# An encoder layer on one core: halved transposes and later squares at the output projection, one more FFN operand made there, and the FFN's first weights in other tiles

## The chip, the cores and the metric

The kernel runs on one core of one Trainium2 chip. The metric is the device time of one execution in microseconds (us). Engines are named as in the profile: PE is TensorE (PEld its weight loads), DVE is VectorE, ACT is ScalarE, POOL is GpSimd, SP is SyncE, which here only issues DMAs.

## The reference, cut to what matters

One layer is applied to a prompt of 2048 rows and to 8 x 16 sample rows (17 tiles of 128 rows; the samples are tile 16). After chunk-band attention and an mLSTM, their outputs are projected and added, and a gated FFN with a causal convolution of width 3 follows, all in float32:

```python
def layer(x, ...):
    h = rms_norm(x, norm_g[0])
    z = h @ w_in                                  # 1024 -> 3592
    ...                                           # att: band attention, mlstm_out: matrix memory
    mix = jnp.concatenate([att, mlstm_out], axis=-1) @ w_out          # 1024 -> 1024
    x = x + rms_norm(mix, norm_g[1])              # "x2" below
    ffn, new_buf = conv_ffn(rms_norm(x, norm_g[2]), conv_buf, w_up, w_conv, b_conv, w_down)
    return x + rms_norm(ffn, norm_g[3]), ...

def conv_ffn(h, buf, w_up, w_conv, b_conv, w_down):
    u = h @ w_up                                  # 1024 -> 5632
    ext = jnp.concatenate([buf, u], axis=1)
    y = b_conv
    for j in range(3):
        y = y + ext[:, j:j + S] * w_conv[j]
    gate, up = jnp.split(y, 2, axis=-1)
    return (gelu(gate) * up) @ w_down, ext[:, S:] # 2816 -> 1024
```

## The kernel before, in words

**Precision.** PE multiplies in fp32r, so every float32 operand is split into a high part (a cast on ACT) and a low part (the operand less its high part, on DVE), and every product is three matmuls: `mm3` issues high x high (L111), high x low (L112) and low x high (L113). A low part is thus wanted right after its high part.

**Stages.** First `w_in` with attention and mLSTM mixed in, then the output projection (`project`), then the FFN in three blocks of rows: block 0 is tiles 0 to 5, block 1 tiles 6 to 11, block 2 the rest. Each block has an up stage over 22 pairs of columns (order 0, 11, 1, 12, ...) and a down stage.

**Output projection.** `project` runs over tiles 0 to 7, 16, 8 to 15. For each it loads the row tile `mr`, normalises half of it, transposes it on PE in eight 128 x 128 pieces (`turn_rows`, which calls `rows_to_T`: PSUM tile `mT_pt`, high part by L218 on ACT and low part by L219 on DVE into `mt`), and multiplies `mt` by `w_out` in two column halves of 24 matmuls each (PSUM tiles `wo_0`, `wo_1`; group `wo`). The result goes through L1057 (DVE, times the norm's gains, into `mx`), L1059 (ACT, the squares), POOL (`rsqrt_mean`) and L1069 (DVE), and is stored as `x2d` (L1070). The code asks for the next tile's transposes after the first column half. `rows_to_T` takes four transposes to a PSUM tile of 512 columns, but all eight to one of 1024 columns if its bank is `ps_big`; tiles 0 to 7 use `ps_mm` (two buffers, which the `wo` sums use too), tiles 16 and 8 to 15 use `ps_big`. In the same time `folds` makes sums of `w_down` on DVE from pieces loaded and stored by POOL's DMAs (groups `fold`, `wtd`).

**FFN operands.** The up stage multiplies 2 x 2 blocks in seven products (P1, P6, P7, P5, then P2, P4, P3, in this order, as Strassen does), each by an operand `B` made of transposed normalised x2. While `project` works on its later tiles, the first block's operands are made by `h2_units(0)` in three units of two tiles: load x2 (`x2r`), squares (L1128, ACT), scale (L1132, DVE), four groups of four transposes (`h2T_pt`, PSUM `ps_sm`, two buffers), and pieces of 512 columns in the ring `quad` ("q", 11 buffers). `EARLY_B = 3`: P1, P6 and P7 are split into `B` at once; the raw pieces of P5, P2, P4 and P3 are stored to DRAM (`lated`) and, when the projection's weights give their space free, loaded again and split whole by `late_B` (L1198 on ACT, L1199 on DVE, 1536 columns each).

**FFN weights.** `load_up` loads the four blocks of `w_up` for a pair of columns; for block 0 it makes the sums s1 to s4 on DVE (L1371) and stores them (`wsd`) for the later blocks. Group n = 0 of a pair of columns has the weights of P1, P6, P7 and P5 (a11, s2, s3, s1), group n = 1 those of P2, P4 and P3 (a12, a22, s4). The split weights (L1353 on ACT, L1354 on DVE) go to `wuh`/`wul` in the pool tags "wh" and "wl" (two buffers each, which `project` uses for `mt` and `mx`) or to the tag "w3" (a set of four tiles in pool `p4`), in turns of three. `low[-1]` is the last low part issued.

**Order.** A list scheduler orders each engine's queue when the kernel is built; what is written earlier goes first where it is ready in the scheduler's own timing. Each engine, SP included, then runs its queue in order. DMAs marked `keep_in_program_order` are not moved. Pool `p4` and the tag "B" tiles in it lie where `w_out` stood (pool `phT`), `p3` lies where the attention's tiles stood (`p1`), and opens before tile 8.

Of the kernel before, what the change touches and what calls it, by code (L numbers as in the profile page):

```python
# [10 lines left out]
F32 = mybir.dt.float32  # L11
# [6 lines left out]
P = 128  # L18
# [3 lines left out]
DB = 8  # L22
# [6 lines left out]
NF = 22  # L29
# [21 lines left out]
def hymba_step(ctx: ExitStack, tc: tile.TileContext, I: dict, O: dict):  # L51
# [97 lines left out]

    gates = const.tile([P, 17, 8], F32, name="gates")  # L150

# [345 lines left out]
    def attention(pair, half):  # L497
        for kg in (2 * half, 2 * half + 1):
            for hh in range(2):
# [4 lines left out]

    tri = const.tile([P, P], F32, name="tri")
    nc.gpsimd.memset(tri, 1.0)
    nc.gpsimd.affine_select(out=tri, in_=tri, pattern=[[1, P]], compare_op=ALU.is_ge, fill=0.0, base=0,
                            channel_multiplier=-1)
    ind = const.tile([P, DB], F32, name="ind")
    nc.gpsimd.memset(ind, 1.0)  # L510
# [443 lines left out]
    wo = []  # L954
    g1 = []
    gatt = const.tile([P, 4], F32, name="gatt")

# [40 lines left out]
    def project(tiles):  # L998
# [27 lines left out]
        def turn_rows(s):  # L1026
            rows_to_T(s.m, s.mt, 0, f"mT{s.t}", ps_mm if s.t < 8 else ps_big)

# [48 lines left out]
    P1, P6, P7, P5, P2, P4, P3 = range(7)  # L1077
    EARLY_B = 3
    ffn = SimpleNamespace(B=[None] * 7, p4=None)

    def open_ffn():
# [10 lines left out]
    def quad(name):  # L1092
        return ffn.p3.tile([P, 512], F32, tag="q", name=name, bufs=11)

# [7 lines left out]
    def h2_units(b, between=(), lead=0):  # L1102
# [3 lines left out]
        def unit(halves, col, n, nm):  # L1106

            rows_ = {}
            for t, _ in halves:
                if t not in rows_:  # L1110
                    rows_[t] = row(f"x2r{t}") if late else rows_tile("xr", [P, D], f"x2r{t}")
                    fetch = nc.sync.dma_start(rows_[t], x2d[t])
                    if late:
                        tc.keep_in_program_order(fetch)
            yield 0.0, 0.0
            if not late:
                yield 0.0, 0.0
# [73 lines left out]

    def late_B():

        for i in (P5, P2, P4, P3):
            new_B(i, 0)
            hi, lo = ffn.B[i][:, 0], ffn.B[i][:, 1]
            nc.sync.dma_start(lo.bitcast(F32), lated[i - EARLY_B])
            nc.scalar.copy(hi, lo.bitcast(F32))  # L1198
            nc.vector.tensor_tensor(lo, lo.bitcast(F32), hi, op=ALU.subtract)  # L1199
# [186 lines left out]
    def load_up(b, i, g, quads=None):  # L1386
        f = ORDERS[b][i]
        n = 2 * i + g
        nm = f"{b}_{f}_{g}"
        if n % 3 < 2:  # L1390
            h = wpool.tile([P, 2112], F32R, tag="wh", name=f"wuh{nm}", bufs=2)
            l = wpool.tile([P, 2112], F32R, tag="wl", name=f"wul{nm}", bufs=2)
            at = [(h[:, i * 512:(i + 1) * 512], l[:, i * 512:(i + 1) * 512]) for i in range(4)]
        else:
            t = [p4.tile([P, 1056], F32R, tag="w3", name=f"wu3{nm}_{i}", bufs=4) for i in range(4)]
            at = [tuple(t[2 * x + i // 2][:, i % 2 * 512:i % 2 * 512 + 512] for x in range(2)) for i in range(4)]
# [95 lines left out]
    pend = [load_up(0, 0, 0)]  # L1492
    late_B()
    pend.append(load_up(0, 0, 1))
    g3 = norm_row(3)
    wcv = p4.tile([P, 44, 4], F32, tag="wcv", name="wcv")
# [13 lines left out]
    for b, tiles in enumerate(FBLOCKS):  # L1510
# [215 lines left out]
        if fast:  # L1726
# [3 lines left out]
            if last:  # L1730
                for i in range(2):
                    sets[i][1] = ps_sm(f"dns{b}_{i}")
                place = lambda pool, i: pool.tile([P, 3, D], F32, tag=f"B{i}", name=f"last{i}", bufs=1)
                fa, xa, fb, xb = place(p3, 0), place(p3, 1), place(p4, 3), place(p4, 4)
                F_ = [fa[:, 0], fa[:, 1], fb[:, 0], fb[:, 1], fa[:, 2]]
# [95 lines left out]
            for p, (_, _, set_, onto) in enumerate(SEQUENCE):  # L1831
                for c in range(3):
# [5 lines left out]
                    elif not last:  # L1838
                        quads = [load_quads(b + 1, 0, i) for i in range(2)]
                        pend = [load_up(b + 1, 0, 0, quads[0])]  # L1840
                    if last and c == 1 and p < 5:
# [37 lines left out]
            while ahead.step():  # L1879
                pass  # L1880
            pend.append(load_up(b + 1, 0, 1, quads[1]))
            continue
        for dh in range(2):
# [9 lines left out]
            for c in range(6):  # L1893
# [5 lines left out]
                elif not last:  # L1899
                    quads = [load_quads(b + 1, 0, i) for i in range(2)]  # L1900
                    pend = [load_up(b + 1, 0, 0, quads[0])]
                ks = list(range(4 * c, 4 * c + (4 if c < 5 else 2)))
# [52 lines left out]
        if not last:  # L1955
            while ahead.step():
                pass
            pend.append(load_up(b + 1, 0, 1, quads[1]))
    nc.sync.dma_start(O["conv_prompt"], halo)
# [94 lines left out]
```

## Time and profile before

| | |
|---|---|
| median of 3 runs (lowest to highest) | 2720.67 us (2716.08 to 2727.13) |
| the profiled execution: its time | 2719.23 us |
| its span, from first to last instruction | 2717.5 us |
| PE busy | 2647.4 us (97%), 16459 matmuls |
| DVE, ACT, POOL busy | 1863.2 (69%), 1422.9 (52%), 693.8 us (26%) |
| granted PE clock, mean | 0.994 |

A row of a view that groups instructions names line, engine, operation and the tiles (out<-in, buffer numbers left out), then the count, busy time and mean duration, and behind the last bar the idle time of the engine just before these instructions, and what ended it. In a timeline the bracket holds the same for one stretch. Matmuls are pipelined: a matmul of 512 columns shows 0.4 us, but the next one starts before it ends, so the spacing of starts is the better measure.

### The profile page before, as it was taken

The numbers are of one execution on the slowest core, as the hardware profiler recorded it, in microseconds if no ns is written. First come the engines' busy times: TensorE is split into PE (matmuls) and PEld (weight loads), VectorE is DVE, ScalarE is ACT, GpSimd is POOL, SyncE is SP. The second block draws the span as 40 slices with busy tenths as digits, with TensorE's granted clock in tenths as the row PEclk, the third lists the DMA queues.
The fourth block names the chain that finished last, engine by engine and source line by source line (L and its number), as shares of the span: only waits on it lengthen the run. The fifth ranks groups of instructions, "written<-read, shape, count | busy, mean of one in ns | idle before, by whom it ended". The sixth has DMA issues, their size and how long they took to land. (4 is left out here: it accounts for less than half of the span.)

```text
span 2717.5 us, 47627 instructions
## 1 busy us (share of the span) xinstructions
PE 2647.4 (97%) x16459; PEld 2475.1 (91%) x16459; DVE 1863.2 (69%) x3519; ACT 1422.9 (52%) x2904; POOL 693.8 (26%) x1325
## 2 busy tenths in 40 slices
PE   7999999999999999999999999999999999999998
PEld 7899989998999998777999997889999888999987
DVE  5444555433556666566899998758888775899866
ACT  4455554433556665333554556654554665555555
POOL 1000001201000001354454542013333212465501
PEclk9999999999999999999999999999999999999999
DMA  5545465458644555588777668767786777788695
GB/s 174 159 123 150 126 184 159 151 157 261 190 141 129 157 147 158 187 291 290 283 235 231 204 199 284 242 195 201 223 221 192 225 251 249 205 246 245 197 345 175
DMA packets 333855, 555.73 MB, mean 205 GB/s; under 512 B 61906, under 2 KB 169518, under 8 KB 333294
## 3 DMA queue, kind: packets, MB, share of 16 engines
q1 hardware_dynamic: 250942, 405.06, 48.0%
q0 software_dynamic: 44080, 113.81, 14.6%
q10 hardware_dynamic: 38592, 33.83, 3.7%
q8 instruction: 129, 2.11, 0.3%
q14 instruction: 112, 0.92, 0.1%
HBM read 390.03 MB, written 172.22 MB: 207 GB/s over the span
## 5 line engine op out<-in xcount | busy, mean ns | idle before, releaser
L111 PE MATMUL uec<-B,wuh 128*128 128x384 f32 (+1 forms) x720 | 235.9, 328 | 6.4 <-DVE ug L1527 4.7
L112 PE MATMUL uec<-B,wuh 128*128 128x384 f32 (+1 forms) x720 | 235.1, 327 | 0.0
L113 PE MATMUL uec<-B,wul 128*128 128x384 f32 (+1 forms) x720 | 234.4, 327 | 0.0
L1353 ACT CAST wuh<-wu 128x512 fp32r<-128x512 f32 x255 | 141.6, 618 | 114.7 <-PE uec L112 110.4
L1354 DVE TENSOR_TENSOR wul<-wu,wuh 128x512 fp32r<-128x512 f32 x255 | 164.3, 683 | 3.0 <-ACT wuh L1353 2.4
L111 PE MATMUL vo<-wi_h,hT 128*128 128x256 f32 x544 | 156.5, 288 | 1.6 <-ACT vo_st L244 1.6
L113 PE MATMUL dn<-wdh,al 128*128 128x512 f32 x385 | 154.5, 401 | 1.0 <-DVE al L1354 0.9
L113 PE MATMUL vo<-wi_h,hT 128*128 128x256 f32 x544 | 155.2, 285 | 0.0
L112 PE MATMUL vo<-wi_l,hT 128*128 128x256 f32 x544 | 155.0, 285 | 0.0
L111 PE MATMUL dn<-wdh,ah 128*128 128x512 f32 x385 | 152.8, 397 | 1.7 <-ACT wdh L1353 1.6
L1354 DVE TENSOR_TENSOR wdl<-wdr,wdh 128x512 fp32r<-128x512 f32 x231 | 145.6, 685 | 9.8 <-ACT wdh L1353 7.8
L112 PE MATMUL dn<-wdl,ah 128*128 128x512 f32 x385 | 151.6, 394 | 0.0
L111 PEld LDWEIGHTS uec<-B,wuh 128*128 128x128 f32 x720 | 135.1, 188 | 9.4 <-issue 4.4
L423 ACT ACTIVATE tmp<-tmp,mn 128x640 f32<-128x640 f32 (+4 forms) x128 | 97.6, 763 | 86.7 <-DVE mn L422 73.9
L422 DVE CUSTOM_DVE_ANT_0 tmp<-s,nb 128x640 f32<-128x640 f32 (+4 forms) x128 | 94.1, 737 | 65.7 <-PE s L412 65.3
L1353 ACT CAST wdh<-wdr 128x512 fp32r<-128x512 f32 x231 | 128.3, 620 | 17.2 <-PE uec L112 7.9
L112 PEld LDWEIGHTS uec<-B,wuh 128*128 128x128 f32 x720 | 135.2, 188 | 0.2
L113 PEld LDWEIGHTS uec<-B,wul 128*128 128x128 f32 x720 | 135.1, 188 | 0.0
L435 DVE TENSOR_TENSOR ptl<-pt,pth 128x640 fp32r<-128x640 f32 (+4 forms) x128 | 93.7, 738 | 58.4 <-ACT pth L434 57.7
L1354 DVE TENSOR_TENSOR al<-ar,ah 128x768 fp32r<-128x768 f32 (+1 forms) x104 | 80.5, 785 | 75.8 <-ACT ah L1353 75.5
L111 PE MATMUL qb<-hT,wi_h 128*128 128x384 f32 (+1 forms) x384 | 128.7, 335 | 0.0
L111 PE MATMUL qk<-hT,wi_h 128*128 128x384 f32 (+1 forms) x384 | 128.0, 333 | 0.6 <-ACT gates L293 0.5
(488 smaller groups left out, 9075.7 us busy)
## 6 DMA issues: line engine op xcount, KB each, us to landing
wu<-in_w_up SPq DMA_DIRECT2D x220, 256.0 KB, 4.8
wu<-wsd SPq DMA_DIRECT2D x176, 256.0 KB, 4.7
wdr<-wtd SPq DMA_DIRECT2D x132, 256.0 KB, 5.9
wi_raw<-in_w_in SPq DMA_DIRECT2D x52, 512.0 KB, 4.1
wdr<-in_w_down SPq DMA_DIRECT2D x99, 256.0 KB, 4.3
wsd<-ws POOLq DMA_DIRECT2D x88, 256.0 KB, 4.8
ar<-ad_S SPq DMA_DIRECT2D x40, 384.0 KB, 3.8
kraw<-kTd SPq DMA_DIRECT2D x112, 128.0 KB, 3.2
```

The source lines that it names most:

```text
L111: nc.tensor.matmul(out, ah, bh, start=start, stop=False, skip_group_check=onto)
L112: nc.tensor.matmul(out, ah, bl, start=False, stop=False, skip_group_check=onto)
L113: nc.tensor.matmul(out, al, bh, start=False, stop=stop, skip_group_check=onto)
L422: nc.vector.tensor_tensor_reduce(o_, s_, b_, 1.0, 3e38, ALU.add, ALU.min, accum_out=mn)
L423: nc.scalar.activation(tmp[:, :n], tmp[:, :n], AF.Exp, bias=mn, scale=-1.0, accum_out=rsum[:, i % 4, hh:hh + 1])
L435: nc.vector.tensor_tensor(s.ptl[:, sl, qc], ptv, s.pth[:, sl, qc], op=ALU.subtract)
L1353: nc.scalar.copy(h, r)
L1354: low.append(nc.vector.tensor_tensor(l, r, h, op=ALU.subtract))
```

## The change: what it does

It does these things:

1. `turn_rows` uses `ps_mm` for tiles 0 to 3 alone (`TURN_BIG = 4`). For the others each group of four transposes takes the first half of a `ps_big` buffer of its own, and L218 and L219 take 512 columns at a time.
2. In `h2_units(0)` the squares of a unit come four steps after the loads of its x2 rows, where it was one.
3. `EARLY_B = 4`: P5's operand is split during the projection too, and lies in `p3`. Three tensors `lated` are left.
4. To make room in `p3`, three of the eleven `quad` buffers lie in `p4` once that exists, and eight in `p3`; `gates`, `tri` and `ind` move from the pool `const` into `pm`, which closes before the FFN.
5. The handoff from the projection to the FFN is written in another order: weights n = 0, then P2's operand, then weights n = 1, then P4's and P3's operands behind the last of these weights. In block 0 the tag "w3" now takes the groups n % 3 == 1 (but the last), "wh"/"wl" the others; in the later blocks it is as before.

```diff
-    gates = const.tile([P, 17, 8], F32, name="gates")
+    gates = pm.tile([P, 17, 8], F32, tag="gates", name="gates", bufs=1)
...
+    TURN_BIG = 4
...
-            rows_to_T(s.m, s.mt, 0, f"mT{s.t}", ps_mm if s.t < 8 else ps_big)
+            rows_to_T(s.m, s.mt, 0, f"mT{s.t}", ps_mm if s.t < TURN_BIG else lambda name: ps_big(name)[:, 0:512])
...
-    EARLY_B = 3
+    EARLY_B = 4
...
     def quad(name):
-        return ffn.p3.tile([P, 512], F32, tag="q", name=name, bufs=11)
+        quads[0] += 1
+        if ffn.p4 is None or quads[0] % 11 < 8:
+            return ffn.p3.tile([P, 512], F32, tag="q", name=name, bufs=8)
+        return ffn.p4.tile([P, 512], F32, tag="q4", name=name, bufs=3)
...
-            yield 0.0, 0.0
-            if not late:
+            for _ in range(4 if late else 2):
                 yield 0.0, 0.0
...
-    def late_B():
-        for i in (P5, P2, P4, P3):
+    def late_B(*which):
+        for i in which:
...
-        if n % 3 < 2:
+        if n % 3 != (2 if b else 1) or n == 2 * NF - 1:
...
     pend = [load_up(0, 0, 0)]
-    late_B()
+    late_B(P2)
     pend.append(load_up(0, 0, 1))
+    with tc.issue_after(low[-1].ins):
+        late_B(P4, P3)
...
-                fa, xa, fb, xb = place(p3, 0), place(p3, 1), place(p4, 3), place(p4, 4)
+                fa, xa, fb, xb = place(p3, 0), place(p3, 1), place(p3, 3), place(p4, 4)
```

The same parts of `gates` hold for `tri` and `ind`; a local list `quads` of the down stages is renamed `raw_up`. In the changed kernel most lines behind `TURN_BIG` stand 1 to 6 lines lower (L1057 is L1058 there, L1353 is L1357).

**The order on the engines.** The rows are those of the built programs, as far as the text speaks of them. First PE where the first unit of `h2_units(0)` begins (`x2r` are its rows), before the change: each group of its transposes stands between matmuls of the projection.

```order
L113 MATMUL wo_1_14868<-wo_13521,mt_14684 128x512
L111 MATMUL wo_1_14868<-wo_13622,mt_14684 128x512
L1140 MATMUL h2T_pt_0_0_14859<-ident,x2r_14769 128x128 x4
L112 MATMUL wo_1_14868<-wo_13622,mt_14684 128x512
L113 MATMUL wo_1_14868<-wo_13622,mt_14684 128x512
```

With the change the unit begins a tile later; three of its four groups and the eight transposes of tile 10 (`mT_pt`) stand in a row between tile 9's last matmul and tile 10's first ones (`mt_14909`), and the two column halves of tile 10 take turns.

```order
L113 MATMUL wo_1_15006<-wo_13622,mt_14788 128x512
L1144 MATMUL h2T_pt_0_0_14933<-ident,x2r_14775 128x128 x4
L1144 MATMUL h2T_pt_1_0_14959<-ident,x2r_14777 128x128 x4
L1144 MATMUL h2T_pt_1_1_14990<-ident,x2r_14777 128x128 x4
L83 MATMUL mT_pt_14974<-ident,mr_14849 128x128 x4
L83 MATMUL mT_pt_14981<-ident,mr_14849 128x128 x4
L1144 MATMUL h2T_pt_0_1_15024<-ident,x2r_14775 128x128 x4
L111 MATMUL wo_0_15069<-wo_13346,mt_14909 128x512
L112 MATMUL wo_0_15069<-wo_13346,mt_14909 128x512
L111 MATMUL wo_1_15134<-wo_13346,mt_14909 128x512
L112 MATMUL wo_1_15134<-wo_13346,mt_14909 128x512
L113 MATMUL wo_0_15069<-wo_13346,mt_14909 128x512
```

The next place is DVE at the transposes of tile 16 (`mt_14574`). Before, its low part, in one instruction, stood behind three additions of `folds`:

```order
L1057 TENSOR_TENSOR mx_14582<-wo_1_14642,norm_row_13058 128x512
L1213 TENSOR_TENSOR fold_2_14395<-fold_0_14330,fold_2_14395 128x512
L733 TENSOR_TENSOR num_14_14159<-num_14_14159,ms_14_1_14186 128x129
L1213 TENSOR_TENSOR fold_3_14397<-fold_3_14397,fold_2_14395 128x512
L667 SCALAR_TENSOR_TENSOR ad_14_14231<-num_14_14159 128x2
L219 TENSOR_TENSOR mt_14574<-mT_pt_14615,mt_14574 128x1024
L668 TENSOR_TENSOR ad_14_14231<-ad_14_14231,colsp 128x2
```

With the change it is in two halves, the first behind one addition:

```order
L1217 TENSOR_TENSOR fold_3_13975<-fold_3_13975,fold_2_13973 128x512
L219 TENSOR_TENSOR mt_14574<-mT_pt_14615,mt_14574 128x512
L722 TENSOR_TENSOR w_14_0_14121<-ms_14_0_14118,w_14_0_14121 128x128
L219 TENSOR_TENSOR mt_14574<-mT_pt_14622,mt_14574 128x512
L1058 TENSOR_TENSOR mx_14582<-wo_1_14645,norm_row_13058 128x512
```

The last place is the handoff, first on DVE, from the last tile's second column half (`mx_15651` before, `mx_15682` now) on. `wul_0_0` are the low parts of weights n = 0, `B_0` the operands of `late_B`. Before:

```order
L1057 TENSOR_TENSOR mx_15651<-wo_1_15684,norm_row_13058 128x512
L1354 TENSOR_TENSOR wul_0_0_15730<-wu_0_15731,wuh_0_0_15729 128x512
L1354 TENSOR_TENSOR wul_0_0_15730<-ws_1_15740,wuh_0_0_15729 128x512
L1354 TENSOR_TENSOR wul_0_0_15730<-ws_2_15741,wuh_0_0_15729 128x512
L1354 TENSOR_TENSOR wul_0_0_15730<-ws_0_15739,wuh_0_0_15729 128x512
L1354 TENSOR_TENSOR wu_11_0_2_15792<-wu_0_15794,wu_11_0_0_15790 128x512
L1371 TENSOR_TENSOR ws_0_15802<-wu_3_15800,wu_2_15798 128x512
L1069 SCALAR_TENSOR_TENSOR mx_15651<-mx_15651,n_15_rs 128x1024
L1371 TENSOR_TENSOR ws_1_15803<-ws_0_15802,wu_0_15794 128x512
L1371 TENSOR_TENSOR ws_2_15804<-wu_0_15794,wu_3_15800 128x512
L1199 TENSOR_TENSOR B_0_15759<-B_0_15759 128x1536
L1679 TENSOR_TENSOR x_0_0_15826<-x_0_0_15825,ub_0_15823 128x384
```

Now three of the four low parts of n = 0 stand ahead of the last tile's instruction, the sums `ws_2` and `ws_3` (whose buffers lie in `p4`) behind it, and the first `B_0` and the last tile's L1070 come after the split of weights n = 1 (`wu_0_1`):

```order
L1358 TENSOR_TENSOR wul_0_0_15761<-wu_0_15762,wuh_0_0_15760 128x512
L1358 TENSOR_TENSOR wul_0_0_15761<-ws_1_15771,wuh_0_0_15760 128x512
L1358 TENSOR_TENSOR wul_0_0_15761<-ws_0_15770,wuh_0_0_15760 128x512
L1058 TENSOR_TENSOR mx_15682<-wo_1_15715,norm_row_13058 128x512
L1375 TENSOR_TENSOR ws_2_15772<-wu_0_15762,wu_3_15768 128x512
L1375 TENSOR_TENSOR ws_3_15773<-wu_1_15764,ws_1_15771 128x512
L1358 TENSOR_TENSOR wu_0_1_2_15796<-wu_1_15764,wu_0_1_0_15794 128x512
L1358 TENSOR_TENSOR wu_0_1_2_15796<-wu_2_15766,wu_0_1_0_15794 128x512
L1375 TENSOR_TENSOR ws_0_15829<-wu_3_15827,wu_2_15825 128x512
L1358 TENSOR_TENSOR wul_0_0_15761<-ws_2_15772,wuh_0_0_15760 128x512
L1358 TENSOR_TENSOR wu_0_1_3_15797<-ws_3_15773,wu_0_1_1_15795 128x512
L1685 TENSOR_TENSOR x_0_0_15853<-x_0_0_15852,ub_0_15850 128x384
```

And SP's queue at the handoff. Before, the four loads of `lated` stood behind tile 14's store of x2:

```order
L1043 DMA mx_15651<-in_x_prompt 128x1024
L1366 DMA wu_2_15798<-in_w_up 128x512
L1366 DMA wu_3_15800<-in_w_up 128x512
L1070 DMA x2d_279<-mx_15550 128x1024
L1197 DMA B_0_15759<-lated_261 128x1536
L1197 DMA B_0_15763<-lated_262 128x1536
L1197 DMA B_0_15767<-lated_263 128x1536
L1197 DMA B_0_15771<-lated_264 128x1536
L105 DMA norm_row_15783<-in_norm_g 128x1024
L1497 DMA wcv<-in_w_conv 128x176
L1499 DMA sext<-in_cache_conv 128x704
L1070 DMA x2d_280<-mx_15651 128x1024
```

Now a load of the second pair's weights, `wu_3_15827`, stands ahead of them. Its buffer is that of a sum of weights n = 0, so it waits for the third `wul_0_0` row of DVE's list above and for POOL's store of that sum:

```order
L1044 DMA mx_15682<-in_x_prompt 128x1024
L1071 DMA x2d_279<-mx_15578 128x1024
L1370 DMA wu_3_15827<-in_w_up 128x512
L1201 DMA B_0_15790<-lated_261 128x1536
L1201 DMA B_0_15804<-lated_262 128x1536
L1201 DMA B_0_15808<-lated_263 128x1536
L105 DMA norm_row_15812<-in_norm_g 128x1024
L1503 DMA wcv<-in_w_conv 128x176
L1505 DMA sext<-in_cache_conv 128x704
L1370 DMA wu_0_15821<-in_w_up 128x512
L1071 DMA x2d_280<-mx_15682 128x1024
```

More of the change, by code (lines that the diff above doesn't have):

```diff
@@ L502, in attention @@
                                              segs=[kg - 1, kg] if kg else [kg]))
-    tri = const.tile([P, P], F32, name="tri")
+    tri = pm.tile([P, P], F32, tag="tri", name="tri", bufs=1)
     nc.gpsimd.memset(tri, 1.0)
@@ L508, in hymba_step @@
                             channel_multiplier=-1)
-    ind = const.tile([P, DB], F32, name="ind")
+    ind = pm.tile([P, DB], F32, tag="ind", name="ind", bufs=1)
     nc.gpsimd.memset(ind, 1.0)
@@ L1077, in hymba_step @@
     P1, P6, P7, P5, P2, P4, P3 = range(7)
-    EARLY_B = 3
+    EARLY_B = 4
     ffn = SimpleNamespace(B=[None] * 7, p4=None)
+    quads = [-1]
     def open_ffn():
@@ L1838, in hymba_step @@
                     elif not last:
-                        quads = [load_quads(b + 1, 0, i) for i in range(2)]
-                        pend = [load_up(b + 1, 0, 0, quads[0])]
+                        raw_up = [load_quads(b + 1, 0, i) for i in range(2)]
+                        pend = [load_up(b + 1, 0, 0, raw_up[0])]
                     if last and c == 1 and p < 5:
@@ L1880, in hymba_step @@
                 pass
-            pend.append(load_up(b + 1, 0, 1, quads[1]))
+            pend.append(load_up(b + 1, 0, 1, raw_up[1]))
             continue
@@ L1899, in hymba_step @@
                 elif not last:
-                    quads = [load_quads(b + 1, 0, i) for i in range(2)]
-                    pend = [load_up(b + 1, 0, 0, quads[0])]
+                    raw_up = [load_quads(b + 1, 0, i) for i in range(2)]
+                    pend = [load_up(b + 1, 0, 0, raw_up[0])]
                 ks = list(range(4 * c, 4 * c + (4 if c < 5 else 2)))
@@ L1957, in hymba_step @@
                 pass
-            pend.append(load_up(b + 1, 0, 1, quads[1]))
+            pend.append(load_up(b + 1, 0, 1, raw_up[1]))
     nc.sync.dma_start(O["conv_prompt"], halo)
```

## The prediction

> **What bounds the kernel now.** I read the page's first part, then the busy time by stage, then PE's rows and waits where the change lies, then the timeline. PE bounds all: it is busy in nearly the whole span, so only time in which it stands still or runs slowly can be gained.
>
> ```profile
> PE 2647.4 (97%) x16459; PEld 2475.1 (91%) x16459; DVE 1863.2 (69%) x3519; ACT 1422.9 (52%) x2904; POOL 693.8 (26%) x1325
> ...
> 1119.60:1300.20 180.60, 169.71 (x792) 135.24 (x791) 107.91 (x173) 64.35 (x153) 87.22 (x161) 0.97 0.82 272
> 1300.20:1340.00 39.80, 37.29 (x202) 36.38 (x201) 38.44 (x56) 22.88 (x33) 15.54 (x21) 0.96 0.75 274
> 1340.00:1640.00 300.00, 294.72 (x1655) 290.63 (x1654) 278.73 (x434) 149.85 (x240) 155.71 (x246) 0.99 0.72 220
> ...
> 1177.00:1184.50 7.50, 6.25 (x15) 4.92 (x16) 4.54 (x10) 0.00 (x0) 6.55 (x12) 0.54 0.88 322
> 1249.00:1252.70 3.70, 3.70 (x9) 2.91 (x10) 1.88 (x3) 0.91 (x1) 2.77 (x5) 0.54 1.03 399
> 1313.90:1317.50 3.60, 3.60 (x14) 3.60 (x13) 3.29 (x2) 0.00 (x0) 0.00 (x0) 0.53 1.01 400
> ```
>
> Columns are the stretch, its length, the busy time (and count) of PE, PEld, DVE, ACT and POOL, the granted PE clock, the DMA share and GB/s. The first stretch is the projection from tile 4's second column half to its end; the next is the handoff, the third the rest of block 0's up stage. In the handoff DVE is busy 38.44 of 39.80 us, and 278.73 of 300 after it: there a late operand is as a rule a late DVE. The last three rows are stretches at half clock.
>
> PE's rows in the projection stretch, with its idle time behind the bar, and the wait ahead of one of the slow stretches:
>
> ```profile
> L111 PE MATMUL wo<-wo,mt 128*128 128x512 f32 x200 | 82.6, 413 | 3.9 <-ACT mt L218 3.2 <-ACT mt L1059 0.4 <-DVE mt L219 0.3
> L113 PE MATMUL wo<-wo,mt 128*128 128x512 f32 x201 | 81.9, 410 | 3.9 <-DVE mt L219 3.7
> L112 PE MATMUL wo<-wo,mt 128*128 128x512 f32 x200 | 81.0, 405 | 0.0
> L83 PE MATMUL mT_pt<-ident,mr 128*128 128x128 f32 x96 | 13.2, 275 | 2.5 <-ACT mx L1059 1.5 <-DVE mr L1023 1.0
> ...
> L716 PE MATMUL ms<-mqk 128*128 128x128 f32 x10 | 2.1, 294 | 0.6 <-DVE num L733 0.6
> ...
> 1244.84 0.39 PE L113 MATMUL wo<-wo,mt 128*128 128x512 f32 x1
> 1245.07 1.03 PE L83 MATMUL mT_pt<-ident,mr 128*128 128x128 f32 x8
> 1247.70 0.50 PE L111 MATMUL wo<-wo,mt 128*128 128x512 f32 x1 [1.60 <-ACT mt L218]
> 1250.26 0.63 PE L113 MATMUL wo<-wo,mt 128*128 128x512 f32 x1
> 1250.68 0.63 PE L111 MATMUL wo<-wo,mt 128*128 128x512 f32 x1
> ...
> 1284.51 1.03 PE L83 MATMUL mT_pt<-ident,mr 128*128 128x128 f32 x8
> 1285.30 0.48 PE L112 MATMUL wo<-wo,mt 128*128 128x512 f32 x1
> ```
>
> Starts are 0.23 us apart for a `wo` matmul (1244.84 to 1245.07) and 0.10 for a transpose (eight from 1284.51 to 1285.30). So 601 `wo` and 191 small matmuls need 140 + 19 = 159 of the 180.6 us; 21 are surplus. Waits make 3.9 + 3.9 + 2.5 + 0.6 = 10.9 of it. Behind the two largest the clock is at 0.54: starts are then 0.42 apart (1250.26, 1250.68). It costs 0.46 of the busy time, 2.9 + 1.7 = 4.6 us. What is left are switches between kinds of matmul. **The projection can give at most 15.5 us.**
>
> By the Trainium skill, page "TensorE: Matmul & The Clock Gate", section "Part 1: The HAM clock gate (the "warmup" mystery)", PE falls to half rate after an idle window of about 3.4 us; here a wait of 1.60 us goes ahead of the stretch at 1249. By that rule the 4.6 us would not go with waits so short, and the sum below would give 2718. The trace speaks for a clock that answers to shorter waits, and I keep the 4.6.
>
> **The change, part by part.** *Halved transposes* (`TURN_BIG`, `ps_big`).
>
> ```profile
> L218 ACT CAST mt<-mT_pt x25: 570/588/1017, 1037.6 to 1285.6; 128x512 fp32r<-128x512 f32 x16, 128x1024 fp32r<-128x1024 f32 x9
> L219 DVE TENSOR_TENSOR mt<-mT_pt,mt x25: 680/692/1225, 1039.3 to 1288.1; 128x512 fp32r<-128x512 f32 x16, 128x1024 fp32r<-128x1024 f32 x9
> ...
> L1157 ACT COPY b<-h2T_pt 128x512 f32<-128x512 f32 x12 | 6.9, 584 | 10.3 <-PE h2T_pt L1140 10.3
> ```
>
> For nine tiles ACT's one cast of 1.02 us becomes two of 0.57, DVE's 1.22 two of 0.68: 9 x 0.12 and 9 x 0.14 us more, beside PE, both engines half idle in this stretch. PE may start after 0.57 + 0.68 where it was 1.02 + 1.22, and the order now puts both column halves' first k's ahead of the second half, 24 matmuls or 5.5 us. For tiles 4 to 7 the waits on `ps_mm` go (the 2.5 us of `mT_pt`). For tile 16, where the largest wait of L219 and the longer slow stretch stand (1177), the new order has 13 matmuls (3 us) between its transposes and its first use, and one addition of `folds` ahead of its low part, not three.
>
> What stays or comes, worked out from the order:
> - Tile 10, at the first unit of `h2_units(0)`: ACT does three copies of 0.58, a cast and a square of about 0.6 each, then the first cast of `mt`: 3.5 us from about 0.4 after tile 9's last matmul. PE has 24 transposes, 2.4 us: a wait of 1.5, and half a chance of a slow stretch (1.7): 2.4.
> - Tile 12: its transposes still stand right behind tile 11's last matmul, the 1.60 of above; the cast is 0.45 shorter: 1.2.
> - Tiles 5 and 8, likewise but with other matmuls between: 0.3 each.
> - `mt` low parts behind additions of `folds` that wait for their loads: not in the trace for this order. Between 0 and 6, nearly twice the 3.7 that L219's waits make in all now; I take 2.1, a little over half of it.
>
> That leaves 6.3, and the gain is 15.5 - 6.3 = **9.2 us**; ends 3 and 14.
>
> *Later squares.* Same instructions, so no busy time. They move the unit a tile later (in tile 10's wait above); its last transposes still stand two tiles, 96 matmuls or 22 us, ahead of the projection's end, so `lated` is full in time. Cost 0.
>
> *P5 made early.* In the projection three more casts and low parts (0.6 and 0.7 us each), three fewer stores: beside PE; without that cover 0.7 each, in the upper end. At the handoff one load of 768 KB, one cast and one low part of 1.75 us fewer.
>
> *The handoff.* Its rows now (T = 1300.2 is the projection's end):
>
> ```profile
> 1293.37 0.33 SPq L1070 DMA_DIRECT2D x2d<-mx  x1
> ...
> 1296.95 4.53 SPq L1197 DMA_DIRECT2D B<-lated  x4
> ...
> 1300.48 0.69 DVE L1057 TENSOR_TENSOR mx<-wo,norm_row 128x512 f32<-128x512 f32 x1
> 1301.09 0.68 DVE L1354 TENSOR_TENSOR wul<-wu,wuh 128x512 fp32r<-128x512 f32 x1
> 1301.69 1.89 DVE L1354 TENSOR_TENSOR wul<-ws,wuh 128x512 fp32r<-128x512 f32 x3
> 1301.82 0.44 PE L113 MATMUL ua<-B,wul 128*128 128x384 f32 x1 [0.40 <-DVE wul L1354]
> 1302.11 0.34 PE L111 MATMUL ua<-B,wuh 128*128 128x384 f32 x1
> 1302.28 0.34 PE L112 MATMUL ua<-B,wuh 128*128 128x384 f32 x1
> 1304.70 1.28 DVE L1069 SCALAR_TENSOR_TENSOR mx<-mx,n_rs 128x1024 f32<-128x1024 f32 x1
> 1306.00 0.33 SPq L1070 DMA_DIRECT2D x2d<-mx  x1
> 1310.43 1.75 DVE L1199 TENSOR_TENSOR B<-B 128x1536 fp32r<-128x1536 f32 x1
> 1312.24 0.44 PE L112 MATMUL ua<-B,wuh 128*128 128x384 f32 x1 [1.96 <-DVE B L1199]
> 1317.79 0.69 DVE L1354 TENSOR_TENSOR wul<-wu,wuh 128x512 fp32r<-128x512 f32 x1 [0.60 <-DMA x2d<-mx]
> ...
> wu<-in_w_up SPq DMA_DIRECT2D x220, 256.0 KB, 4.8
> x2d<-mx SPq DMA_DIRECT2D x17, 512.0 KB, 7.9
> ```
>
> Before, PE waits 0.40, 1.96 for P2's operand, and loses 1.7 at the clock of 0.53: 4.1. (The last DVE row waits for tile 15's store of x2, issued at 1306.00: 11.8 us.) Now, each step by these rows:
> - `wul` of n = 0 needs the buffer of tile 14's `mx`, free at T + 0.9 at the latest; three low parts of 0.63 end at T + 2.8. Only then does SP get past `wu_3` of the second pair, which stands ahead of the loads of `lated`; those went out from T - 3.3 on, now from T + 3. `wu_3` lands 4.8 us later, T + 7.6.
> - DVE does L1057, two sums, two low parts by T + 5.9, waits for `wu_3`, makes its sum, and only then the fourth low part: T + 8.9. PE needs that for P7 at T + 5.5 (22 matmuls at 0.17 after its 0.4): a wait of 3.4.
> - P2's operand comes after a low part, an addition, L1069 and its own 1.75: T + 13.0; PE is there at T + 11: 2.0 (or a slow stretch in its place).
> - The second pair's first low part needs the buffer of tile 15's `mx`: L1069 ends at T + 11.3, where it was T + 5.8; with the median landing of 7.9 T + 19.3, while DVE's own list ends at T + 18.9. PE has P2, P5 and six high parts until T + 17.8: 1.7.
>
> Sum 0.4 + 3.4 + 2.0 + 1.7 = 7.5 against 4.1: **3.4 us lost**. Ends: if `wu_3` lands while DVE is busy and P5's 1.75 us is all gained, 1 us won; if tile 15's store again takes 11.8 and the clock drops once more, 9 lost.
>
> *Weights in "w3".* The same three sets in another phase; the last group, forced into "wh", follows a use of that buffer by one group. 0. *Eight and three `quad` buffers*: eleven in turns as before; what it costs is `wu_3` above. *`gates`, `tri`, `ind`*: addresses only, 0.
>
> *Rest of block 0* is ordered anew by the same rules, and PE waits there for DVE:
>
> ```profile
> PE uec L111 <- DVE ug L1527: 4.7, 4, 2.1
> ```
>
> With its share of two slow stretches some 8 us could go or come again: 0, ends -4 and +4.
>
> **Sum.** The profiled execution took 2719.23 us, 1.4 below the median of the runs. 2719.2 - 9.2 + 3.4 = 2713.4; I say **2713.5 us**.
>
> **Rivals.**
> - *Faster*: the handoff's waits hide and block 0's go too. 13 off in the projection, 1 at the handoff, 4 in block 0: 2701. For it: DVE loses 1.75 us of work where it is fullest. Against it: SP's queue. Chance 0.22.
> - *Slower, SP held at `wu_3`*: everything behind it, the three loads of `lated` and tile 15's store, shifts with it, and each us that it stands longer than I say costs DVE and so PE nearly a us. It decides from 9 us lost on; with 14 the time is 2724. Against it: weights are landing in 4.8 us as a rule. Chance 0.13.
> - *The slow stretches don't hang on short waits*: 4.6 stay, 2718. Against it: the stretch at 1249 has a wait right ahead of it, and 1.60 us was enough. Chance 0.08. (The Trainium skill's page on the clock gate, named above, has that rule.)
> - *The change does nothing*: in-order queues put new waits where old ones were; ACT waits for `x2r`, DVE for `folds`. 2719 to 2722. Chance 0.07.
>
> The forecast has 0.50; its own range is 2707 to 2721. The time is in 2702 to 2727 with 8 in 10: down to the faster case's middle, up to the slower one's. 0.5% is 13.6 us, about what a measurement of this kernel can tell from no change: faster means under 2707, slower over 2734. Most of the faster case and a little of the forecast give 0.24, a third of the slower one 0.05; same 0.71.
>
> **What would show it.** PE's waits for `mt` in the projection falling from 7.8 us (L111, L113) to 4 or 5, those of `mT_pt` to about 0; a wait at tile 10; no clock under 0.9 near tile 16. At the handoff a wait for P7's low weights of about 3 us, the loads of `lated` issued after the projection's end, and 20 us from there to the second pair's first low part. Wrong would be a handoff without the P7 wait, a projection that keeps its waits, or a block 0 that changes by more than 4 us.

## The result: 0.3% slower, with the profile after

The changed kernel takes 2729.96 us (median of 13 runs, 2725.86 to 2732.49), the kernel before 2720.8 (13 runs as well): ratio 1.0030, 95% interval 1.0021 to 1.0039, 9 us slower. The forecast was 2713.5, 7 us faster, with 2727 as its upper end.

First the page's first part and then the busy time by stage, before and now. Columns as in the prediction: the stretch, its length, busy time (and count) of PE, PEld, DVE, ACT and POOL, clock, DMA share, GB/s. The eight stages are all up to the projection, the projection, the handoff (261 matmuls from number 8839 on), the rest of block 0's up stage, its down stage, block 1's up and down stage, and the rest. Before:

```profile
8.40:1044.40 1036.00, 1009.21 (x7665) 980.97 (x7666) 542.56 (x1342) 536.56 (x1303) 83.58 (x224) 1.00 0.54 160
1044.40:1300.20 255.80, 241.16 (x1177) 195.01 (x1176) 150.59 (x268) 97.62 (x244) 109.37 (x207) 0.98 0.74 243
1300.20:1350.50 50.30, 47.79 (x263) 46.88 (x262) 48.83 (x72) 28.85 (x44) 20.89 (x30) 0.97 0.73 261
1350.50:1633.70 283.20, 277.92 (x1564) 274.59 (x1564) 262.90 (x410) 140.21 (x225) 148.15 (x234) 0.99 0.72 220
1633.70:1806.00 172.30, 170.57 (x760) 138.22 (x761) 124.65 (x184) 112.03 (x202) 25.76 (x45) 1.00 0.79 251
1806.00:2125.70 319.70, 319.21 (x1830) 318.64 (x1828) 262.66 (x396) 162.38 (x270) 106.23 (x195) 1.00 0.72 204
2125.70:2296.90 171.20, 170.97 (x761) 137.47 (x762) 122.86 (x185) 108.15 (x199) 29.74 (x46) 1.00 0.77 250
2296.90:2717.50 420.60, 410.60 (x2448) 383.27 (x2446) 346.15 (x662) 234.68 (x420) 167.46 (x329) 1.00 0.77 236
```

With the change:

```profile
PE 2653.5 (97%) x16459; PEld 2480.5 (91%) x16459; DVE 1864.0 (68%) x3530; ACT 1423.2 (52%) x2915; POOL 691.7 (25%) x1325
...
9.20:1050.00 1040.80, 1015.80 (x7665) 987.14 (x7666) 541.65 (x1341) 535.39 (x1301) 82.00 (x224) 1.00 0.53 159
1050.00:1295.90 245.90, 236.17 (x1176) 193.59 (x1176) 152.59 (x281) 101.33 (x259) 108.72 (x205) 0.99 0.73 246
1295.90:1351.60 55.70, 49.97 (x263) 48.20 (x262) 48.88 (x74) 27.07 (x41) 21.55 (x33) 0.94 0.73 247
1351.60:1634.10 282.50, 276.57 (x1564) 272.75 (x1564) 262.06 (x408) 141.20 (x227) 145.16 (x230) 1.00 0.71 217
1634.10:1808.60 174.50, 171.02 (x763) 138.24 (x762) 125.40 (x184) 110.12 (x200) 31.83 (x47) 1.00 0.78 252
1808.60:2129.60 321.00, 320.47 (x1831) 319.93 (x1829) 262.88 (x396) 162.49 (x270) 105.03 (x195) 1.00 0.72 202
2129.60:2303.90 174.30, 172.14 (x760) 137.25 (x761) 122.40 (x185) 108.13 (x199) 26.36 (x46) 1.00 0.76 245
2303.90:2725.70 421.80, 411.32 (x2448) 383.44 (x2446) 346.13 (x662) 234.93 (x420) 168.42 (x329) 0.99 0.77 235
```

The projection is 9.9 us shorter and the handoff 5.4 longer: the two terms that the forecast speaks of (9.2 and 3.4) are there. The rest of block 0 is 0.7 shorter. What turns the sign lies where the forecast put nothing: 4.8 us before the projection, 2.2 and 3.1 in two down stages, 1.3 in block 1's up stage, 1.2 behind, and 0.8 ahead of the first matmul. PE is 6.1 us longer *busy* (2647.4 to 2653.5) with the same 16459 matmuls, 6.6 of it ahead of the projection. One more half-clock stretch there (three, before two) is 1.6 of that; the rest is not waiting but slower matmuls.

In the projection (from the second column half of tile 4 on) PE's rows, the two halves of `mt`, and tile 10:

```profile
L111 PE MATMUL wo<-wo,mt 128*128 128x512 f32 x211 | 85.1, 403 | 2.4 <-ACT mt L218 2.2 <-ACT mt L1060 0.2
L113 PE MATMUL wo<-wo,mt 128*128 128x512 f32 x212 | 83.7, 398 | 0.4 <-DVE mt L219 0.3
L83 PE MATMUL mT_pt<-ident,mr 128*128 128x128 f32 x96 | 13.8, 284 | 1.0 <-DVE mr L1024 1.0
L1144 PE MATMUL h2T_pt<-ident,x2r 128*128 128x128 f32 x48 | 7.2, 286 | 2.2 <-DVE x2r L1136 2.2
...
L218 ACT CAST mt<-mT_pt x34: 572/587/609, 1043.1 to 1283.4; 128x512 fp32r<-128x512 f32 x34
L219 DVE TENSOR_TENSOR mt<-mT_pt,mt x34: 678/682/693, 1044.8 to 1284.1; 128x512 fp32r<-128x512 f32 x34
...
1211.02 0.63 PE L1144 MATMUL h2T_pt<-ident,x2r 128*128 128x128 f32 x4 [0.24 <-DVE x2r L1136]
1213.60 1.09 PE L1144 MATMUL h2T_pt<-ident,x2r 128*128 128x128 f32 x8 [1.95 <-DVE x2r L1136]
1215.73 1.88 PE L83 MATMUL mT_pt<-ident,mr 128*128 128x128 f32 x8 [1.03 <-DVE mr L1024]
```

The 7.8 us of waits for `mt` are 2.8 now, those of `mT_pt` 1.0 where they were 2.5. The tile 10 wait is there, 3.2 us in three pieces, and behind it the one half-clock stretch left in the projection (1215.9, 3.4 us).

The handoff (T = 1295.9): SP's issues, DVE's low parts, PE's waits.

```profile
1297.15 0.33 SPq L1370 DMA_DIRECT2D wu<-in_w_up  x1
1297.58 1.33 SPq L1201 DMA_DIRECT2D B<-lated  x3
1301.01 0.65 SPq L1370 DMA_DIRECT2D wu<-in_w_up  x1
...
1301.31 0.68 DVE L1358 TENSOR_TENSOR wul<-ws,wuh 128x512 fp32r<-128x512 f32 x1
1304.84 1.76 DVE L1203 TENSOR_TENSOR B<-B 128x1536 fp32r<-128x1536 f32 x1 [0.59 <-ACT B L1202]
1315.75 0.68 DVE L1358 TENSOR_TENSOR wul<-wu,wuh 128x512 fp32r<-128x512 f32 x1
...
1302.05 0.45 PE L113 MATMUL uec<-B,wul 128*128 128x384 f32 x1 [1.45 <-DVE wul L1358]
1304.86 0.44 PE L111 MATMUL ua<-B,wu 128*128 128x384 f32 x1 [0.80 <-ACT B L1202]
1306.65 0.45 PE L112 MATMUL ua<-B,wu 128*128 128x384 f32 x1 [1.35 <-DVE B L1203]
1314.61 0.50 PE L111 MATMUL ua<-B,wuh 128*128 128x384 f32 x1 [2.12 <-ACT wuh L1357]
...
1307.90:1311.50 3.60, 3.60 (x14) 3.60 (x13) 2.26 (x2) 1.47 (x1) 0.00 (x0) 0.53 1.02 404
1314.80:1318.30 3.50, 3.50 (x11) 2.96 (x11) 3.50 (x7) 3.02 (x6) 2.03 (x4) 0.51 0.94 328
```

SP stands at the second pair's `wu_3` (1297.15) until T + 1.2, and the loads of `lated` go out behind it, at T + 1.7; before, it was T - 3.3. P7's low part starts at T + 5.4, P2's at T + 8.9, and the second pair's first one at T + 19.9. PE waits 5.7 us (2.4 before) and two stretches run at half clock (one before). The last of these waits is for ACT's cast of the second pair's first weights: their load (1301.01) went out behind those of `lated`, and ACT waited for it until 1313.94, 12.9 us later, where these loads take 4.3 us as a median.

### The profile page after: what moved, and what is told of

It reads as the page before. It is cut to its first block, busy times and chain, and to the rows that moved or that the text cites. A ratio compares the mean times of both kernels' runs of the same rounds, so it can differ in the third digit from the quotient of the medians.

```text
span 2725.7 us, 47647 instructions
## 1 busy us (share of the span) xinstructions
PE 2653.5 (97%) x16459; PEld 2480.5 (91%) x16459; DVE 1864.0 (68%) x3530; ACT 1423.2 (52%) x2915; POOL 691.7 (25%) x1325
## 4 chain that ended last, share of the span: by engine, by line
PE 43%; DVE 4%; DMA 3%; issue 1%; POOL 1%; ACT 1%; SPq 0%; DVEq 0%; POOLq 0%; ACTq 0%
PE uec L111 5%; PE uec L113 5%; PE uec L112 5%; PE dn L113 3%; PE dn L111 3%; PE dn L112 3%; PE ua L113 3%; PE ua L111 3%; PE ua L112 3%; PE dnm L113 1%; PE dnm L112 1%; PE dnm L111 1%; PE ub L111 1%; PE ub L113 1%; PE ub L112 1%
## 5 line engine op out<-in xcount | busy, mean ns | idle before, releaser
L1357 ACT CAST wuh<-wu 128x512 fp32r<-128x512 f32 x255 | 141.6, 617 | 105.6 <-PE uec L112 100.2
L1357 ACT CAST wdh<-wdr 128x512 fp32r<-128x512 f32 x231 | 127.8, 620 | 19.6 <-DMA wdr<-in_w_down 6.3
```

The source lines that it names most:

```text
L1357: nc.scalar.copy(h, r)
```

## The experiments

Each was timed beside the kernel before on one chip; the ratio is to that, with its 95% interval. The stages are those of above, from one profile each, in us. "Padded" is the changed kernel with 64 bytes more, explained below. One profile is one execution: the changed kernel's two differ by 1.8 us in the projection and 2.2 in block 0's down stage. A difference of about 2 us between two stages of the table is thus no more than a hint, unless it comes again.

```
kernel                              ratio [interval]          proj. handoff rest  down0  up1   down1
before                              1                         255.7  50.3  283.2  172.3 319.7  171.1
changed                             1.0030 [1.0021, 1.0039]   245.9  55.7  282.5  174.5 321.0  174.4
changed, second time                1.0023 [1.0010, 1.0036]   247.7  55.5  282.7  172.3 321.0  173.2
before + gates, tri, ind in pm      1.0023 [1.0013, 1.0033]   254.3  50.7  279.6  172.3 321.1  171.3
padded (changed + 64 bytes)         1.0009 [0.9998, 1.0020]   244.6  55.2  284.1  171.3 319.7  172.4
before + 32 bytes                   1.0006 [0.9994, 1.0018]   252.2  50.6  282.0  172.7 320.6  171.0
before + halved transposes          0.9979 [0.9966, 0.9992]   248.0  50.1  279.2  171.8 319.7  171.4
  ... and later squares             0.9990 [0.9979, 1.0000]   245.9  51.3  280.5  173.1 319.7  171.2
padded + wu_3 behind lated          0.9988 [0.9977, 1.0000]   245.0  50.9  282.9  172.7 319.7  172.7
padded + quad count set back        0.9967 [0.9953, 0.9980]   244.3  52.5  278.6  171.3 319.7  172.3
  ... and old phase of w3           0.9955 [0.9942, 0.9968]   245.0  51.7  279.0  170.5 319.8  171.9
      that, whole transposes        0.9982 [0.9969, 0.9994]   252.1  53.6  277.4  172.0 319.8  171.3
      that, early squares           0.9968 [0.9955, 0.9980]   248.5  53.3  276.5  171.2 319.8  171.8
      that, 32 bytes more           0.9967 [0.9954, 0.9980]   244.0  53.5  277.4  171.1 320.5  172.3
```

**Addresses alone.** The theory: `gates`, `tri` and `ind`, gone from `const`, shift all pools behind it by 1088 bytes, and matmuls read from there at another pace. The rival: one execution's scatter.

```diff
-    gates = const.tile([P, 17, 8], F32, name="gates")
+    gates = pm.tile([P, 17, 8], F32, tag="gates", name="gates", bufs=1)
(tri and ind alike)
```

> The kernel before, with one part of the change alone: gates, tri and ind in pool pm, not const. The order on every engine is that of the kernel before; every tile of wpool, pr, pa and small lies 1088 bytes lower. Theory of addresses: the 5.6 us that the changed kernel loses before its output projection (1044.5 to 1050.1 us) come from these addresses; the middle spacing of 384-column matmuls rises from 175 to 177 ns there, the projection starts 4 to 6 us later and the time is 5 us above the kernel before. Theory of scatter (the loss was that one execution's): spacing 175 ns, within 2 us of the kernel before.

The ratio is 1.0023, 6.2 us (interval 3.5 to 9.0). In its profile the projection starts only 1.6 us later than before (1046.1), not 4 to 6, since PE waited 4.5 us less on the way there. As a whole that stage is no measure: in the nine profiles of kernels with `wi_h` where it was or 1024 bytes off it takes 1032.3 to 1042.8 us. Less PE's waits, and 1.6 us for each piece of half clock, these nine take 996.6 to 1000.2 us, and the three profiles with `gates`, `tri` and `ind` in `pm` and no padding 1002.2 to 1002.9. Two rows from the timeline of each kernel, the first and last of a run of matmuls without a gap, 24 in the kernel before and 23 in this one:

```profile
467.60 0.33 PE L111 MATMUL qb<-hT,wi_h 128*128 128x384 f32 x1
471.59 0.34 PE L113 MATMUL qb<-hT,wi_l 128*128 128x384 f32 x1
```

```profile
470.65 0.34 PE L112 MATMUL qb<-hT,wi_h 128*128 128x384 f32 x1
474.53 0.34 PE L113 MATMUL qb<-hT,wi_l 128*128 128x384 f32 x1
```

3.99 us in 23 steps is 173.5 ns, 3.88 in 22 steps 176.4. The same queues, the same instructions, `hT` at the same address (147424); `wi_h` at 11392 in place of 12480. (In these matmuls `hT` is the moving operand and `wi_h` the stationary one, which L270 gives first; the 256-column ones, L286, have it the other way round.)

The other way round, the changed kernel with its addresses moved back by 64 bytes:

```diff
-    nhalf = const.tile([P, 8], F32, name="nhalf")
+    nhalf = const.tile([P, 24], F32, name="nhalf")[:, 0:8]
```

> The changed kernel with nhalf 64 bytes longer, so that the tiles of wpool, pr, pa and small lie 1024 bytes lower than in the kernel before, not 1088; the order on every engine is that of the changed kernel. If what slows the first stage is an address modulo something up to 1024, the spacing goes back to 175 ns and the time falls by 5 us, to about 2725. If it is the address as such, or no address at all, it stays within 2 us of the changed kernel, at 2730.

1.0009, where the changed kernel had 1.0030 and 1.0023: 64 bytes give back 4 to 6 us, by the spacings too. And a third place, 32 bytes more in the kernel before (`[P, 16]` in the line above):

> The kernel before with nhalf 32 bytes longer; order on every engine unchanged, and wi_h of the first stage at 12512, which is 32 modulo 64 (before: 12480, 64 modulo 128; changed kernel: 11392, 0 modulo 128). If what counts is that the moving operand starts at a multiple of 128 bytes, the spacing of the 384-column matmuls stays at 175 ns. If it counts whether it starts like the other operand hT (147424, 32 modulo 64), it changes: 177 or more if alike is bad, under 175 if alike is good. Time within 3 us of the kernel before in the first case, 5 us and more off in the second.

All starts of one matmul to the next of its width, by place of `wi_h` (ns; median, in brackets the mean of those under 300):

```
wi_h modulo 128            first stage, 384 col.  256 col.       projection, 512   block 1 up, 384
64 (before)                175 (179.3)            118 (123.0)    234 (233.2)       174 (174.3)
64 (padded)                175 (179.1)            118 (123.2)    234 (233.2)       174 (174.3)
 0 (changed)               177 (181.5)            119 (123.6)    232 (233.4)       174 (175.0)
 0 (before + pm)           177 (181.4)            119 (123.6)    232 (233.5)       174 (175.0)
96 (before + 32 bytes)     174 (179.6)            120 (124.0)    227 (228.4)       174 (174.8)
96 (the last row above)    174 (179.3)            120 (124.0)    227 (228.0)       174 (174.7)
```

Kernels with one remainder agree, whatever their order; the seven others with 64 are within 0.4 ns of its rows. (128 is a label here: the addresses in the rows of 64, and in those of 96, differ by 1024, those in the rows of 0 not at all, so 256, 512 or 1024 would fit as well.) From 64 to 0 it is 1742 x 2.1 + 2589 x 0.5 + 1819 x 0.7 ns = 3.7 + 1.3 + 1.3 = 6.3 us, beside the measured 6.2; block 0's up stage, not counted, adds about 1 (176.1 against 175.4 ns, 1562 starts). From 64 to 96 the projection wins 770 x 4.8 ns = 3.7 us (252.2) and the first stage loses 2.5, block 1's 0.9: 1.0006. Of the two guesses about what counts, neither is right as put: 32 modulo 64 was good for one width and bad for another. And the guess takes `wi_h` for the moving operand, which it is at 256 columns alone. At 384 columns, and in the projection (`mt`), the operand that was shifted is the stationary one, while the moving one (`hT`, `wo`) stayed where it was: there it is the stationary operand's place that sets the pace. Why is open.

**The changed kernel again**, for what of its profile was that execution's:

> The changed kernel once more, for a second profile. What is of the program comes again: the spacing of 177 ns in the first stage, the projection at 245 to 247 us, the handoff (261 matmuls from number 8839 on) at 54 to 57. Open are the down stages: block 0's took 174.5 us and block 1's 174.4 in the first profile, 172.3 and 171.1 in the kernel before, 171.3 and 172.4 in the padded kernel, whose order is the same. If that loss is of the addresses, both come out at 173.5 or more again; if it was that execution's, nearer to 172. Half-clock stretches: each should follow a piece of 3.41 us, counted in one fixed grid through the whole execution, in which PE stood still for over 1.5 us.

The spacings, the handoff (55.5) and block 1's up stage (321.0) come again; block 0's down stage does not (172.3), so the 2.2 us there was scatter. Block 1's down stage is 2.1 longer again; it is 0.2 to 1.6 longer in the padded kernels and at most 0.3 in those made from the kernel before. By the traces 0.8 of it is pace: its 512-column matmuls start 233.1 ns apart in both profiles of the changed kernel, 231.8 to 231.9 in the kernel before and the padded one (670 starts). The rest is waits of PE for `ah`, `al` and `x2r`, 2.1 and 1.6 us, where the kernel before has none; what in the order makes these late was not run apart. The 1.5 us of the last guess is too high: 1.25 was enough once (last section).

**Halved transposes alone, and with the later squares** (the lines of the change itself, `TURN_BIG = 4`, then `range(4 if late else 2)`):

> The kernel before with the halved transposes alone (TURN_BIG = 4). By the prediction's sum the projection gives 9.2 us less what tile 10 keeps; addresses, handoff and operands are as before. The projection, 255.5 us before, takes 245 to 248, and the time is 7 to 10 us below the kernel before. The theory that new waits take the place of the old ones: within 3 us. Theory that the later program pays it back (the order is made anew from there on): projection 246, but block 0 longer by 4 us or more.

> The same with the later squares too. By the prediction they cost nothing: within 1.5 us of the run with the halved transposes alone, the projection at 245 to 248 us. Rival: they are what takes the wait for ACT out at tile 10, and the projection is 2 us or more shorter than with the halved transposes alone.

7.7 us off the projection, ratio 0.9979 (5.7 us, under the 7 to 10 expected, with an interval of 2.2 to 9.2): the mechanism stands, on its own too, and later stages give nothing back. With the squares the projection is another 2.1 shorter, but the ratio is 0.9990; by time alone the two can't be told apart. The pair was run once more on the best kernel below, once with the transposes and once with the squares put back:

> The kernel of the best run so far (padded by 64 bytes, the count of quad buffers set back, old phase of w3: 0.9955 of the kernel before, projection 245.0 us) with the transposes as before the change (1024 columns at a time, tiles 0 to 7 in ps_mm). By the prediction the halved transposes give 9.2 us: the projection is 253 to 256 us and the time 7 to 10 us longer, ratio about 0.999. Rival: the later squares and the new order had their part in it: projection 248 to 251, ratio 0.997.

> The same kernel with the squares as early as before the change, the halved transposes kept. Prediction's step (the later squares cost and bring nothing): within 2 us of it, projection 244 to 246. Rival from the run of the halved transposes alone (projection 248.0 without, 245.9 with the later squares): projection 2 us longer, ratio 0.9963.

The projection is 252.1 without the halved transposes (7.1 longer) and 248.5 without the later squares (3.5 longer); ratios 0.9982 and 0.9968 against 0.9955. What the two parts save is PE's waits and half-clock pieces, at 1.6 us a piece. In the four profiles without halved transposes these cost 16.1 to 19.2 us in the projection, in the two with them alone 13.4 and 14.4, in the eight with both 10.2 to 13.9. So the halved transposes' gain is shown; the 2 to 3.5 us of the later squares are likely, as they come in both pairs, but not clear of the scatter, and in the time not separated.

**The handoff: SP held at `wu_3`.** The theory was the prediction's: `wu_3` of the second pair holds the loads of `lated`. Padded, with this load allowed only behind them:

```diff
-                nc.sync.dma_start(q[i], src(i))
+                if f == ORDERS[0][1] and i == 3:
+                    with tc.issue_after(ffn.late.ins):    # the last load of lated
+                        nc.sync.dma_start(q[i], src(i))
+                else:
+                    nc.sync.dma_start(q[i], src(i))
```

> The changed kernel with the 64 bytes of the run before (called the padded kernel: its handoff, 55.2 us over the 261 matmuls from number 8839 on, is 4.9 longer than before), and one edge more: the load wu_3 of the second pair may go out only after the loads of lated, so SP is not held at it. Theory of the held queue: the loads of lated go out about 3 us ahead of the projection's end, the waits for P2's operand (0.6 + 1.4) and the half-clock stretch behind them go, and the handoff is 2 to 4 us shorter than in the padded kernel. Theory that DVE's list sets the handoff: P2's operand waits as long as before for DVE, or the second pair's weights wait longer since wu_3 now lands later; within 1 us of the padded kernel.

SP's rows in the padded kernel (T = 1288.3), and then in this one (T = 1293.2) with two of PE's four waits left there (the others, 0.74 and 1.02, are for `uu` and for a cast of later weights):

```profile
1288.85 0.33 SPq L1370 DMA_DIRECT2D wu<-in_w_up  x1
1289.27 1.33 SPq L1201 DMA_DIRECT2D B<-lated  x3
```

```profile
1289.93 4.32 SPq L1201 DMA_DIRECT2D B<-lated  x3
1298.12 0.59 SPq L1372 DMA_DIRECT2D wu<-in_w_up  x1
...
1298.63 0.45 PE L113 MATMUL uec<-B,wul 128*128 128x384 f32 x1 [0.70 <-DVE wul L1358]
1302.64 0.44 PE L112 MATMUL ua<-B,wu 128*128 128x384 f32 x1 [1.84 <-DVE B L1203]
```

The loads go out from T - 3.3 on, the padded kernel's wait of 3.7 us at the second pair's first weights is gone, the half clock too, and the handoff is 50.9 in place of 55.2: the held queue cost 4.3 us, of which 1.6 is the half clock; in the time it is 0.2% (1.0009 to 0.9988; the intervals just meet). P2's operand hardly gains (1.84 against 0.63 + 1.35): there the rival holds, DVE's list was full.

**The handoff: the buffers in `p4`.** These exist only from T on. The count of `quad` buffers set back puts the first pair's four sums into `p3`:

```diff
+    quads[0] = -1
     pend = [load_up(0, 0, 0)]
```

> The padded kernel with the count of quad buffers set back to its start at the handoff, so that all four sums of the first pair lie in p3, and the three buffers in p4 take wu_0, wu_1, wu_2 of the second pair. If the buffers in p4, which exist only from the projection's end on, are what makes P7's low part late, its wait (1.0 in the padded kernel, 1.45 in the changed one) goes, and the loads of lated go out earlier, since wu_3 waits for less: handoff 2 to 4 us shorter. Rival: the wait moves to the second pair, whose loads are now late (3.7 us there in the padded kernel becomes 6 or more), and the handoff is as long or longer.

Now `wu_3` stands ahead of tile 14's store of x2, and SP is not held behind it (the loads of `lated` start at T - 3.3). P7's wait is gone, P2's operand waits 2.7, the handoff is 52.5. More comes behind it: from matmul 10000 to block 0's end PE waits nowhere (115.5 us, 120.1 padded, 120.3 before). Ratio 0.9967, 0.4% under the padded kernel's 1.0009, the largest step of all these runs. The order on the engines is made anew behind this edit, so how the buffers act so far behind the handoff is not shown. With block 0's "w3" in its old phase besides (`if n % 3 < 2`):

> The same, and block 0's weights in the tiles of w3 in the old phase (n % 3 == 2), so that weights n = 1 go to wh and wl and DVE makes their low parts after P2's operand, not ahead of it. Prediction's step (the phase costs 0): within 1 us of the run with the count set back alone. Rival: DVE is relieved by three low parts (1.9 us) ahead of P2's operand, and the handoff is 1 to 2 us shorter.

0.9955, the best; its handoff is 0.8 us shorter, with a half-clock piece less (1.6 us). The intervals overlap, so the phase is worth nothing to some 3 us. That kernel with 32 bytes more:

> The same kernel as the best run so far with 96 bytes in place of 64, so that the tiles of wpool lie 32 bytes higher (wi_h at 11488, 96 modulo 128, as in the run with 32 bytes more of the kernel before, where 512-column matmuls of the projection were 227 ns apart, 384-column ones of the first stage 174, 256-column ones 120). If these spacings hang on the address modulo 128 alone, they come again: projection 241 to 242 us, 3.5 shorter, first stage within 1 us, block 1's up stage 0.9 longer: time 2 to 4 us lower, ratio 0.994. Rival: they hang on more than that, and the projection stays at 245.

The spacings come as foretold (two rows of an unbroken run of 17, 3.63 us in 16 steps, 227 ns), the time does not fall as expected: 0.9967. A half-clock stretch at tile 10 takes back what the projection wins (244.0), and the first stage loses its 2.2.

```profile
1220.82 0.39 PE L111 MATMUL wo<-wo,mt 128*128 128x512 f32 x1
1224.45 0.39 PE L112 MATMUL wo<-wo,mt 128*128 128x512 f32 x1
```

## Why the prediction was wrong, by its own steps

The forecast was 7.2 us under the kernel before, the measured time is 9.2 over it: 16.4 us apart. Two terms that only place tiles make up most of it.

- **"`gates`, `tri`, `ind`: addresses only, 0": the first step that failed.** It is worth +6 us, shown alone (1.0023) and undone (1.0009, 4 to 6 us back). With it the forecast of 2713.5 would have been about 2720, at the kernel before.
- **"Eight and three `quad` buffers: eleven in turns as before; what it costs is `wu_3` above": the second.** With their count set back the ratio goes from 1.0009 to 0.9967, some 11 us, where the prediction had priced `wu_3` within the handoff's 3.4. By the profiles 2.7 us of it lie in the handoff and 5.5 in the rest of block 0, which the prediction put at 0. The held queue is part of it (0.9988 with that alone undone). With both steps undone the kernel is 9.0 us under the kernel before, which is what the projection was to give.
- **The projection, -9.2:** -9.9 in the first profile, -8.0 in the second; the halved transposes alone make 7.7, and putting them back costs 7.1. Right, and by its mechanism: waits for `mt` 2.8 (4 or 5 foretold), `mT_pt` 1.0, no slow stretch at tile 16 in any profile of the changed kernel. At tile 10 the wait was put down to ACT; it is DVE's scaling of `x2r` and `mr`, 3.2 us and a slow stretch where 2.4 in all were taken.
- **"Later squares. Cost 0":** they cost nothing, and seem to bring 2 to 3.5 us in the projection; if so, part of the 9.2 was theirs.
- **The handoff, +3.4:** +5.4 and +5.2, inside its ends (1 won, 9 lost). The chain was right in its first links: SP is held at `wu_3` for DVE's `wul`, `lated` goes out behind T (T + 1.7, T + 3 foretold), and P7's low part is late: 1.45 (3.4 foretold, but `wu_3` landed by T + 4.8, not T + 7.6, and DVE stood 0.6 us for it). P2's 2.15 (2.0) is 0.80 for ACT's cast and 1.35 for DVE. The second pair's 2.12 (1.7; 0.56 in the second profile) came out near by luck: it was put down to the low part, whose buffer waits for tile 15's store, and the first low part did start at T + 19.9 (20); but PE stood for the high part before it, whose load was under way for 12.9 us behind those of `lated`. Left out was the clock: the waits, 5.7, are shorter than the 7.5 of the sum, but two stretches at half clock, 1.6 us each, stood only in its far end (9 lost). The rival *SP held at `wu_3`* was thus at work within the forecast.
- **"Weights in w3: 0":** at most 3 us.
- **Rest of block 0, 0 ± 4:** -0.7. **The later stages, not in the sum:** +1.3 in block 1's up stage is of the addresses; of the 2 to 3 in its down stage 0.8 is pace, the rest is waits whose cause stays open; block 0's 2.2 did not come again.
- **The rival that slow stretches don't hang on short waits:** refuted, see the last section.

In the first pair of profiles the named terms give -9.9 + 5.4 - 0.7 = -5.2 where -5.8 was foretold. That agreement is partly luck: the profiled execution before has 283.2 us in the rest of block 0, with two half-clock pieces, where the four other kernels with the old handoff have 279.2 to 282.0. The forecast priced the lines that move work, and put those that only place tiles at nothing or too low.

## What to carry to other kernels

Price a tile that moves between pools like a change of code: look up which operands of the busiest matmuls shift, the stationary ones too, and measure one pad of 32 and one of 64 bytes, before the profiles of two versions are compared. Compare the matmuls' spacing, not the length of a stage in one profile, which here scattered by more than the effect. When buffers of a ring are placed in a pool that opens late, follow which load reuses which buffer, for SP, which issues in order, held everything behind that load here (4.3 us). And with PE at 97%, count a wait of 2 us as up to 3.6: the slow stretch behind it (1.6) goes on the bill.

## What the runs showed of the hardware that was not expected

**The matmul's pace hangs on where an operand starts, the stationary one too.** The table above: 384 columns 174 to 177 ns, 256 columns 118 to 120, 512 columns 227 to 234, for three places of `wi_h` and `mt`, with none that is best for all widths.

**The half clock answers to idle time within a fixed grid.** In each of the 14 profiles the half-clock stretches begin at one phase of a grid of 3413.3 ns, to 5 ns, through the whole execution. With the profiles cut at this grid (from 20 to 2690 us), PE's idle time in a piece decides on the next one, and it takes less to stay at half clock than to get there:

```
clock and idle time of a piece of 3.41 us    pieces    next piece at half clock
full, under 1.2 us                            10687       0
full, 1.2 to 1.85 us                            124      10
full, over 1.85 us                               60      60
half, under 0.6 us                               70       0
half, 0.6 to 1.45 us                             11      11
```

So a wait of 2 us costs 1.6 more or nothing, as it falls into one piece or over the border of two, which differs from execution to execution. That may be part of the scatter of the runs (2715 to 2729 for the kernel before), which was not shown. The Trainium skill, page "TensorE: Matmul & The Clock Gate", section "Part 1: The HAM clock gate (the "warmup" mystery)", has a free-running window of 3413 ns, which these profiles bear out; by its table an idle window is needed for the fall to half rate, and here 1.25 us of idle time in a piece were enough at the least and 1.83 the most that passed. The two differ, and for this kernel the measurement decides.
